# Three chunks of a layer's first MLP product computed by Strassen's scheme with split fp32 operands

## The chip, the core and the metric

The kernel runs on one core of a Trainium2 chip. The metric is the device time of one execution in microseconds (us): the median of the runs shown. TensorE does the matrix products and is fed with weights by a load step of its own (PE and PEld in the profile), VectorE (DVE) and ScalarE (ACT) work element by element, GpSimd (POOL) and SyncE (SP) issue transfers; SP's queue carries nearly all loads of weights.

## The reference

One inference step of a model of two layers. The 640 tokens (512 of a latent grid, 128 of a prompt) have 1024 features. Each layer computes

```python
hn = rmsnorm(x, w0) * (1 + scale1) + shift1
y  = mixer(hn)                       # attention, gated convolution, RG-LRU, pooling; then w_out
x  = x + gate1 * y
hn = rmsnorm(x, w1) * (1 + scale2) + shift2
x  = x + gate2 * (square(relu(hn @ w_mlp1)) @ w_mlp2)
```

with `w_mlp1` of 1024 x 4096 and `w_mlp2` of 4096 x 1024, all in fp32. The modulations (`shift`, `scale`, `gate`) come from products with `w_ada`. The results are the normalized tokens, and the keys, values and states of the prompt.

## The kernel before

Activations lie with features on the 128 partitions and tokens along the row. They are handled in two halves of 320 tokens, A and B (the code's `c`). Products keep fp32 accuracy by splitting each operand x into a rounded part `hi` and the rest `lo = x - hi`, and adding three products: w_hi x_hi + w_lo x_hi + w_hi x_lo. A **group** (line 574) is one output tile of 128 features x 320 tokens: 8 blocks of 128 input features, three matmuls each, 24 in all, in one of two PSUM banks of the pool `gp`. An evacuation (`evac`) follows each group; the next but one group takes the bank.

Weights come as tiles `st` of 512 x 256 (512 KB), loaded by SP into a ring of 3 buffers (`load_next`, line 217). `step` (line 237) turns a tile into a pair: ScalarE casts it to `wh` (line 260), VectorE computes `wl = st - wh` (line 243). Four pairs are held at a time.

The MLP of a layer runs in 4 chunks `q` of 1024 hidden features. Chunk q of the first product, "1" in the names of groups, is 16 groups (4 keys `b` of 256 features, two tiles `mi` each, halves A and B). Its evacuation `evac1` (line 1266) is a relu and a square into `z` (hi) on ScalarE, and a square and a subtraction into `z` (lo) on VectorE (lines 1275 to 1280). Then chunk q of the second product, "2" in the names, is another 16 groups whose evacuation adds to the residual `x` on VectorE (line 1219). So the tensor engine alternates between 1-chunks and 2-chunks.

What engine does what when is settled at build time. Python generators are advanced by `tick` and emit instructions, and a scheduler then sets the order of each engine's instructions by its own estimate, with some raised in priority. At run time each engine works through its list in that order and waits where a semaphore says so; a waiting instruction holds up all that stand behind it on its engine. Names in the rows drop the numbers of buffers.

Of the kernel before, what the change touches and what calls it, by code (L numbers as in the profile page):

```python
# [9 lines left out]
F32 = mybir.dt.float32  # L10
# [29 lines left out]
AP2 = (0, 2, 4, 6, 8)  # L40
AQ = (0, 1, 3, 5)
AP1 = {"xr": (0, 8), "xb": (8, 16)}
RP = 645
XC = 642
UP = 643
# [49 lines left out]
class Slots:  # L95
# [14 lines left out]
    def put(self, *tiles):  # L110
        for t in tiles:
            self.free.append(self.own.pop(id(t))[0])


class Net:
    def __init__(self, tc, es, ins, outs, consts):
        self.tc, self.nc, self.I, self.O = tc, tc.nc, ins, outs
        nc = self.nc
        self.gens = []
        self.c0 = CUT[0]  # L120
        self.const = es.enter_context(tc.tile_pool(name="const", bufs=1))
# [19 lines left out]
        self.stage, self.ready, self.half = {}, {}, None  # L141
        self.ada_acc, self.ada_k = [None, None], 0
        self.setup_consts(consts)

    def setup_consts(self, consts):
        nc, c = self.nc, self.const
        self.cst = c.tile([P, 164], F32, name="cst")
        nc.scalar.dma_start(self.cst, consts[:, 0:164])
        self.ident = self.cst[:, 0:128]
        self.inv = self.cst[:, 128:130]  # L150
        self.edge = self.cst[:, 130:162].rearrange("p (f j) -> p f j", f=2)
        self.consts = consts
        self.sel = c.tile([P, 2], F32, name="sel")
        selv = self.cst[:, 0:128].rearrange("p (j r) -> p r j", j=4)[:, 0:2, :]
# [12 lines left out]
        self.plw = c.tile([P, 2, P], F32, name="plw")  # L167
        self.kcT = c.tile([P, 2, P], F32, name="kcT")
        self.vsb = c.tile([P, 6, 256], F32, name="vsb")
        self.osb = c.tile([P, 2, T], F32, name="osb")  # L170
# [46 lines left out]
    def load_next(self):  # L217
        if self.loaded >= len(self.items):
            return
        kind, src = self.items[self.loaded][:2]  # L220
        nc = self.nc
        t = self.wst.tile([P, 1024], F32, tag="st", name=f"st{self.loaded}")
        if kind == "w":
# [13 lines left out]
    def step(self):  # L237
        nc = self.nc
        if self.half is not None:
            key, st, wh, wl, i = self.half  # L240
            with self.tc.high_priority(offset=self.offw(key)):
                eng = nc.gpsimd if self.booting else nc.vector
                eng.tensor_tensor(wl.rearrange("p k c -> p (k c)"), st,  # L243
                                  wh.bitcast(F32).rearrange("p k c -> p (k c)"), OP.subtract)
            self.ready[key] = (wh, wl)
            self.half = None
            self.load_next()
            return True
        if self.ii >= len(self.items):
            return False  # L250
        it = self.items[self.ii]
        if it[0] == "w":
            if self.live >= 4:
                return False
            self.live += 1
            st = self.stage.pop(self.ii)
            wh = self.whl.tile([P, 4, 256], F32R, tag="wh", name=f"wh{self.ii}")
            wl = self.whl.tile([P, 4, 256], F32R, tag="wl", name=f"wl{self.ii}")
            with self.tc.high_priority(offset=self.offw(it[2])):
                nc.scalar.copy(wh.rearrange("p k c -> p (k c)"), st)  # L260
            self.half = (it[2], st, wh, wl, self.ii)
            self.ii += 1
            return True
        if it[0] == "d":
# [16 lines left out]
        self.load_next()  # L281
        self.load_next()
        if (k, j2) == (KT - 1, 1):
            self.spawn(self.ada_fin(l, s, self.ada_ps), first=True)
        return True

    def ada_dve(self, l, s, g, kp):
        nc = self.nc
# [19 lines left out]
            return True  # L308
        self.stage.pop(self.ii)
        self.ii += 1  # L310
        self.load_next()
        if fin:
            ps = self.psU.get()
            for o in range(2):
# [771 lines left out]
    def layer(self, l, last):  # L1086
# [175 lines left out]
        for q in range(4):  # L1262
# [28 lines left out]
            self.gemm(self.order([(L, "1", q, b) for b in range(4)], lambda i: q == 0 and i == 0), self.mov_h,  # L1291
                      evac1, pre=pre1)
            if q == 0 and not last:
                derive()
            self.tick()
# [241 lines left out]
    def run(self):  # L1537
# [3 lines left out]
        for l in range(DEPTH):  # L1541
# [18 lines left out]
            ni = 0  # L1560
            for q in range(4):
                for b in range(4):
                    it += self.w_items(I["w_mlp1"][l], (L, "1", q, b), 0, 1024 * q + 256 * b)
                    n = 2 if q else AQ[b]
                    it += nxt[ni:ni + n]
                    ni += n
# [43 lines left out]
```

## Time and profile before

| | us |
|---|---|
| median of 3 runs (lowest, highest) | 1478.43 (1477.95, 1479.59) |
| the profiled execution | 1477.53 |
| its span, first to last instruction | 1475.4 |
| VectorE busy in the span | 940.5 (64%) |
| ScalarE busy in the span | 588.2 (40%) |

The profile's page gives for each engine the time in which it was busy and its share of the span. The rows further down come from that page and from questions put to the trace: groups of instructions with their mean time, stretches of time with the busy time of each engine in them, and instructions in order of time with the idle time ahead of each and what ended it.

### The profile page before, as it was taken

How to read it: one execution, taken by the hardware profiler on the slowest of the kernel's cores; microseconds unless marked ns; L12 is line 12 of the kernel's file. 1: busy time of each engine (PE TensorE's matmuls, PEld its weight loads, DVE VectorE, ACT ScalarE, POOL GpSimd, SP SyncE). 2: the span in 40 equal slices, each digit the busy share in tenths (PEclk: the TensorE clock that was granted, in tenths of full speed). 3: DMA queues.
4: the chain of work that ended last, by engine and by line, in shares of the span. 5: the costliest groups of instructions: out<-in, count | busy, mean ns of one | idle time of the engine just before them, and what ended most of it. 6: DMA issues, size and time to landing. Idle time of an engine off the chain costs nothing.

```text
span 1475.4 us, 24595 instructions
## 1 busy us (share of the span) xinstructions
PE 1451.5 (98%) x9991; PEld 1388.8 (94%) x9991; DVE 940.5 (64%) x1846; ACT 588.2 (40%) x1077; POOL 60.9 (4%) x104
## 2 busy tenths in 40 slices
PE   8999999999999999999999999999999999999998
PEld 6877989999999999999999999899999999999997
DVE  5655989898886677766468778848434433433453
ACT  5535784353224123224245578526412312312321
POOL 1221010010000000000002200000000000000000
PEclk9999999999999999999999999999999999999999
DMA  9586112434554444544134411211222122222211
GB/s 332 177 220 185 59 54 88 149 98 157 187 170 130 157 137 137 171 142 129 58 104 123 128 31 57 72 58 58 90 82 86 58 86 75 69 86 64 80 44 72
DMA packets 135960, 164.59 MB, mean 112 GB/s; under 512 B 10212, under 2 KB 111032, under 8 KB 135848
## 3 DMA queue, kind: packets, MB, share of 16 engines
q1 hardware_dynamic: 131256, 156.41, 34.8%
q0 software_dynamic: 4224, 6.45, 1.8%
q8 instruction: 79, 1.29, 0.4%
q14 instruction: 33, 0.27, 0.1%
q10 hardware_dynamic: 368, 0.16, 0.0%
HBM read 150.40 MB, written 3.15 MB: 104 GB/s over the span
## 4 chain that ended last, share of the span: by engine, by line
PE 85%; DVE 6%; issue 4%; DMA 3%; ACT 1%; SPq 0%; DVEq 0%; ACTq 0%; POOLq 0%
PE g_L_1A L583 15%; PE g_L_0A L583 15%; PE g_L_0B L583 14%; PE g_L_1B L583 14%; PE g_L_o_0B L583 1%; PE g_L_o_1B L583 1%; PE g_L_v L1176 1%; PE TB L840 1%; PE U L948 1%; PE S L793 1%; PE g_L_o_0A L583 1%; PE g_L_o_1A L583 1%; PE TA L820 1%; PE U L278 1%; DMA st<-in_w_in 1%
## 5 line engine op out<-in xcount | busy, mean ns | idle before, releaser
L260 ACT CAST wh<-st 128x1024 fp32r<-128x1024 f32 x180 | 188.8, 1049 | 337.4 <-PE g_L_1B L583 275.7
L243 DVE TENSOR_TENSOR wl<-st,wh 128x1024 fp32r<-128x1024 f32 x176 | 215.0, 1222 | 102.8 <-ACT wh L260 102.4
L1279 DVE TENSOR_TENSOR e<-e 128x320 f32<-128x320 f32 x128 | 62.4, 488 | 109.9 <-ACT z L1276 109.5
L583 PE MATMUL g_L_1A<-z,wh 128*128 128x320 f32 (+1 forms) x512 | 121.4, 314 | 0.0
L583 PE MATMUL g_L_0A<-z,wh 128*128 128x320 f32 (+1 forms) x512 | 120.7, 314 | 0.0
L583 PE MATMUL g_L_0B<-z,wh 128*128 128x320 f32 (+1 forms) x512 | 117.2, 309 | 2.3 <-DVE x L1219 2.2
L583 PE MATMUL g_L_1B<-z,wh 128*128 128x320 f32 (+1 forms) x512 | 115.7, 306 | 0.0
L305 DVE SCALAR_TENSOR_TENSOR m<-st,SC,m 128x512 f32<-128x512 f32 x112 | 79.5, 746 | 26.3 <-DMA st<-in_w_ada 26.3
L583 PEld LDWEIGHTS g_L_0B<-z,wh 128*128 128x128 f32 x512 | 87.4, 191 | 2.8 <-DVE x L1219 2.8
L583 PEld LDWEIGHTS g_L_1A<-z,wh 128*128 128x128 f32 x512 | 87.7, 188 | 2.5 <-issue 2.5
L583 PEld LDWEIGHTS g_L_0A<-z,wh 128*128 128x128 f32 x512 | 87.8, 188 | 0.1
L583 PEld LDWEIGHTS g_L_1B<-z,wh 128*128 128x128 f32 x512 | 86.4, 189 | 0.1
L305 DVE SCALAR_TENSOR_TENSOR pt<-st,SC,pt 128x512 f32<-128x512 f32 x112 | 79.9, 745 | 3.4 <-DMA st<-in_w_ada 2.9
L583 PE MATMUL g_L_1A<-hh,wh 128*128 128x320 f32 x256 | 80.0, 313 | 0.0
L583 PE MATMUL g_L_1A<-z,wl 128*128 128x320 f32 (+1 forms) x256 | 79.9, 312 | 0.0
L583 PE MATMUL g_L_0A<-z,wl 128*128 128x320 f32 (+1 forms) x256 | 79.9, 312 | 0.0
L583 PE MATMUL g_L_0A<-hh,wh 128*128 128x320 f32 x256 | 79.5, 311 | 0.2
L583 PE MATMUL g_L_0B<-hl,wh 128*128 128x320 f32 x256 | 79.3, 310 | 0.0
L583 PE MATMUL g_L_1A<-hl,wh 128*128 128x320 f32 x256 | 79.2, 309 | 0.0
L583 PE MATMUL g_L_0A<-hl,wh 128*128 128x320 f32 x256 | 79.1, 309 | 0.0
L583 PE MATMUL g_L_0B<-hh,wh 128*128 128x320 f32 x256 | 79.1, 309 | 0.0
L583 PE MATMUL g_L_1B<-hh,wh 128*128 128x320 f32 x256 | 79.1, 309 | 0.0
(587 smaller groups left out, 3969.9 us busy)
## 6 DMA issues: line engine op xcount, KB each, us to landing
st<-in_w_mlp SPq DMA_DIRECT2D x128, 512.0 KB
st<-in_w_ada SPq DMA_DIRECT2D x80, 512.0 KB
st<-in_w_in SPq DMA_DIRECT2D x36, 512.0 KB
st<-in_w_out SPq DMA_DIRECT2D x16, 512.0 KB
z<-in_w_ada SPq DMA_DIRECT2D x24, 256.0 KB
z<-qk POOLq DMA_DIRECT2D x32, 80.0 KB, 4.4
z<-qk SPq DMA_DIRECT2D x32, 80.0 KB
xt<-in_x_sample SPq DMA_DIRECT2D x4, 512.0 KB
```

What stands on the lines that cost most here:

```text
L243: eng.tensor_tensor(wl.rearrange("p k c -> p (k c)"), st, wh.bitcast(F32).rearrange("p k c -> p (k c)"), OP.subtract)
L260: nc.scalar.copy(wh.rearrange("p k c -> p (k c)"), st)
L278: nc.tensor.matmul(self.ada_ps[32 * g:32 * g + 32, :], self.SC[:, k, :], src[:, (g % 2) * 512:(g % 2 + 1) * 512], start=(k == 0), stop=(k ...
L305: nc.vector.scalar_tensor_tensor(acc[:, 0:512], w, col, acc[:, 0:512], OP.mult, OP.add)
L583: nc.tensor.matmul(pt[:, 0:ncols], w[:, k % 4, sl], r, start=(n == 0), stop=(n == 23))
L793: nc.tensor.matmul(ps[:, o:o + b - a], Q[:, qt * P:(qt + 1) * P], K[:, a:b], start=True, stop=True)
L820: nc.tensor.transpose(ta[:, kt * P:(kt + 1) * P], es[0][:, kt * P:(kt + 1) * P], self.ident)
L840: nc.tensor.matmul(tb[64 * j:64 * j + 64, 0:P], self.vsb[:, kt, (h - 1 + j) * 64:(h + j) * 64], self.pTs[j][:, kt * P:(kt + 1) * P], start ...
L948: nc.tensor.matmul(u[:, 0:321], self.rgw[:, 4 * d + 2 * g + f, :], xc[:, cs], start=True, stop=True)
L1176: nc.tensor.matmul(pt[:, 0:256], a[:, k, ts], b[:, k % 4, :], start=(n == 0), stop=(n == 23))
L1279: nc.vector.tensor_tensor(r[:, 0:n], r[:, 0:n], r[:, 0:n], OP.mult)
```

## The change

In layer 2 the 1-chunks q = 1, 2 and 3 (`FAST`) are computed by Strassen's scheme (Winograd's form). The block of a half chunk, 1024 input features x 512 hidden features x 640 tokens, is cut in two along each dimension. In place of 8 products of half blocks there are 7, numbered `prod`, each of 24 matmuls (2 tiles `mi`, 4 blocks of 128 input features, three matmuls). A half chunk runs them in the order 1, 5, 6, 3, 2, 7, 4.

- **Sums of activations.** While chunk 0 of the second product runs, `sums_gen` makes the four sums and differences of token halves, each split in hi and lo, in buffers that are free at that time: for each of 4 blocks of features 12 instructions on VectorE and 4 on ScalarE.
- **Sums of weights.** Each half chunk loads 7 tiles: A11, A21, A22, A12, B11, B21, B22. Four products take a sum that VectorE adds in place (line 311), and each of the seven operands is split as before (lines 314 and 252).
- **Evacuation.** Products 1, 5 and 6 are copied out of PSUM by ScalarE while their banks go on to accumulate (6 on top of 1; 3 on 5; 7 on 6; 4 on 7); 3, 2 and 7 are added to these copies by VectorE (line 450). The final relu, the two squares and the subtraction follow in `late`. Six banks take part: two of `gp`, the three of the tile `S`, and `TB`.
- **Ring.** Tiles are loaded into 5 buffers. `spent` loads the next tile once the tile five places before it is used up. The scratch memory for transfers that GpSimd issues is set to 8192 bytes per partition.

The core of the diff:

```diff
+WST = 5
+FAST = {(1, 1), (1, 2), (1, 3)}
...
-        self.wst = es.enter_context(tc.tile_pool(name="wst", bufs=3))
+        self.wst = es.enter_context(tc.tile_pool(name="wst", bufs=WST))
...
+    def spent(self, *items):
+        self.gone.update(items)
+        while self.loaded < len(self.items) and (self.loaded < WST or self.loaded - WST in self.gone):
+            self.load_next()
...
+    def sum_and_split(self, it):
...
+        dst, add, prod, done = todo[self.micro]
+        st = self.held[dst][0]
+        if add:
+            nc.vector.tensor_tensor(st, st, self.held[add][0], OP.add)
...
+        nc.scalar.copy(wh.rearrange("p k c -> p (k c)"), st)
+        self.half = ((key + (prod,), 0), st, wh, wl, [self.held.pop(n)[1] for n in done])
...
+    def fast_items(self, w, key, r0, c0):
+        out = []
+        for name, i, j, todo in (("A11", 0, 0, [("A11", None, 1, [])]), ("A21", 1, 0, []),
+                                 ("A22", 1, 1, [("A21", "A22", 5, ["A22"]), ("A11", "A21", 6, ["A21"])]),
+                                 ("A12", 0, 1, [("A11", "A12", 3, ["A11"]), ("A12", None, 2, ["A12"])]),
+                                 ("B11", 0, 0, []), ("B21", 1, 0, [("B11", "B21", 7, ["B11", "B21"])]),
+                                 ("B22", 1, 1, [("B22", None, 4, ["B22"])])):
+            out.append(("x", w[r0 + 512 * j:r0 + 512 * j + 512, c0 + 512 * i:c0 + 512 * i + 256], name, todo, key))
+        return out
...
+    def sums_gen(self):
...
+        for k in range(4):
...
+            full(b12, k, B)
+            full(w, k, A)
+            tt(t1, w, b12, OP.subtract)
+            yield
+            split(T1[k], t1)
+            full(b22, k + 4, B)
+            yield
+            tt(w, b22, b12, OP.subtract)
+            split(T3[k], w)
...
+    def fast_mlp1(self, l, q, put):
...
+        pairs = [(g[0], g[1]), (S[:, 0:512], S[:, 512:1024]), (S[:, 1024:1536], tb)]
...
+            def late():
+                if sign:
+                    nc.scalar.activation(v, v, AF.Relu, scale=sign)
+                nc.scalar.activation(hi, v, AF.Square)
+                nc.scalar.activation(v, v, AF.Square)
+                yield
+                nc.vector.tensor_tensor(lo, v, hi.bitcast(F32), OP.subtract)
...
+        for b in range(2):
+            Y, Z, X = pairs[b % 3], pairs[(b + 1) % 3], pairs[(b + 2) % 3]
+            r = u2 = None
+            for prod, bank in ((1, Y), (5, Z), (6, Y), (3, Z), (2, X), (7, Y), (4, Y)):
...
+                fresh = prod in (1, 5, 2)
+                for mi in range(2):
...
+                    for k in range(4):
+                        hi, lo = self.Tsum[prod][k]
+                        for w, x in ((wh, hi), (wl, hi), (wh, lo)):
+                            nc.tensor.matmul(bank[mi][:, 0:HC], w[:, k, sl], x, start=(fresh and n == 0), stop=(n == 11),
+                                             skip_group_check=not fresh)
+                            n += 1
...
+                        if prod in (1, 5, 6):
+                            nc.scalar.copy(half({1: t1, 5: t5, 6: u2}[prod], mi), p)
+                        elif prod == 4:
+                            nc.scalar.activation(half(r, mi), p, AF.Relu, scale=-1.0)
+                        else:
+                            nc.vector.tensor_tensor(half(r, mi), p, half({3: u2, 2: t1, 7: t5}[prod], mi), OP.add)
...
-    nc = bacc.Bacc("TRN2", target_bir_lowering=False, num_devices=1)
+    nc = bacc.Bacc("TRN2", target_bir_lowering=False, num_devices=1, dynamic_dma_scratch_size=8192)
```

The places in the order of instructions of which the prediction speaks are three. On VectorE, from the end of chunk 0 of the second product into chunk 1 of the first, before the change:

```order
L1219 SCALAR_TENSOR_TENSOR x_76<-g_L1_2_3_0_1B_11711,mod1_92,x_76 128x128
L243 TENSOR_TENSOR wl215_11775<-st215_11519,wh215_11774 128x1024 [waits DMAHW5_49,Activation_49]
L1279 TENSOR_TENSOR e1_226_11771<-e1_226_11771 128x320 [waits Activation_49]
L1280 TENSOR_TENSOR z11_206_11770<-e1_226_11771,z13_205_11769 128x320 [waits DVE_49]
L1279 TENSOR_TENSOR e0_227_11809<-e0_227_11809 128x320 [waits Activation_49]
L1280 TENSOR_TENSOR z6_208_11808<-e0_227_11809,z2_207_11807 128x320 [waits DVE_49]
L1279 TENSOR_TENSOR e2_228_11839<-e2_228_11839 128x320 [waits Activation_49]
L1280 TENSOR_TENSOR z11_206_11770<-e2_228_11839,z13_205_11769 128x320 [waits DVE_49]
```

and with the change from the second weight tile that is split in the fast chunk on; the names end in the product, `wl215_2` is the `wl` of product 2, `st220` and `st221` are A21 and A22 of the second half chunk, `st223` and `st224` its B11 and B21, and `e1_235` takes product 3:

```order
L252 TENSOR_TENSOR wl215_2_11890<-st215_11589,wh215_2_11889 128x1024 [waits PE_49,Activation_49]
L252 TENSOR_TENSOR wl217_7_11924<-st216_11628,wh217_7_11923 128x1024 [waits PE_49,Activation_49]
L311 TENSOR_TENSOR st220_11907<-st220_11907,st221_11943 128x1024 [waits DMAHW3_49,DMAHW2_49,DVE_49]
L252 TENSOR_TENSOR wl218_4_11966<-st218_11872,wh218_4_11965 128x1024 [waits DMAHW0_49,PE_49,Activation_49]
L450 TENSOR_TENSOR e1_235_11938<-S_36_11819,e2_234_11904 128x320 [waits PE_49]
L411 TENSOR_TENSOR z11_206_11941<-e1_235_11938,z13_205_11940 128x320 [waits Activation_49]
L450 TENSOR_TENSOR e1_235_11938<-S_36_11819,e2_234_11904 128x320 [waits PE_49]
L450 TENSOR_TENSOR e0_236_11984<-TB_72_11820,pt1_65_11823 128x320 [waits PE_49]
L252 TENSOR_TENSOR wl219_1_12007<-st219_11874,wh219_1_12006 128x1024 [waits DMAHW1_49,Activation_49]
L311 TENSOR_TENSOR st223_11987<-st223_11987,st224_12141 128x1024 [waits DMAHW6_49,DMAHW5_49,DVE_49]
```

Where evacuation arithmetic and two subtractions for weights stood, there now stand two additions that wait for transfers (DMAHW) ahead of the sums that empty PSUM.

On TensorE in the same half chunk, with the change. The tile `S` holds three banks; the first rows are the end of product 5's first tile (bank 0 of `S`), then come four matmuls of product 6 (two of them in one row), then product 5's second tile (bank 1 of `S`):

```order
L432 MATMUL S_36_11819<-osb_2_11272,wl214_5_11732 128x320
L432 MATMUL S_36_11819<-vsb_2_11273,wh214_5_11731 128x320
L432 MATMUL f1_0_11821<-qk_6_11274,wh214_6_11816 128x320 [waits Activation_49]
L432 MATMUL f1_0_11821<-qk_6_11274,wl214_6_11817 128x320
L432 MATMUL f1_0_11821<-qk_6_11274,wh214_6_11816 128x320 x2
L432 MATMUL S_36_11819<-osb_2_11272,wh214_5_11731 128x320 [waits Activation_49]
L432 MATMUL S_36_11819<-osb_2_11272,wl214_5_11732 128x320
```

Twelve matmuls of one output tile no longer stand in one piece: the second tile of product 5 waits for ScalarE's copy of the first, which lies in another bank of the same `S`, and four matmuls of product 6 have been put ahead of it.

On VectorE in chunk 0 of the second product, where before only evacuations (line 1219, now 1404) and subtractions for weights stood, with the change the sums of activations and of weights (`st213`, `st214` are A21 and A22) stand between evacuations:

```order
L381 TENSOR_TENSOR e2_231_11464<-e2_231_11464 128x320 [waits DVE_49]
L354 TENSOR_TENSOR e0_230_11463<-hh_77,hl_78 128x320 [waits DVE_49]
L363 TENSOR_TENSOR hl_78<-e0_230_11463,hh_77 128x320 [waits Activation_49]
L360 SCALAR_TENSOR_TENSOR qk_6_11274<-e2_231_11464,qk_6_11274 128x320 [waits Activation_49]
L385 TENSOR_TENSOR e0_230_11463<-e2_231_11464,e0_230_11463 128x320 [waits DVE_49]
L311 TENSOR_TENSOR st213_11442<-st213_11442,st214_11482 128x1024 [waits DMAHW4_49,DMAHW3_49]
L1404 SCALAR_TENSOR_TENSOR x_76<-g_L1_2_1_0_1A_11468,mod1_92,x_76 128x320 [waits PE_49]
L363 TENSOR_TENSOR m5_123_11278<-e0_230_11463,m3_121_11276 128x320 [waits Activation_49]
```

Between the evacuations of two groups there are now some seven to nine instructions.

## Rows read from the trace of the kernel before

**Rows 1.** the page: TensorE's busy time, and the chain that ended last.
```profile
PE 1451.5 (98%) x9991; PEld 1388.8 (94%) x9991; DVE 940.5 (64%) x1846; ACT 588.2 (40%) x1077; POOL 60.9 (4%) x104
PE 85%; DVE 6%; issue 4%; DMA 3%; ACT 1%; SPq 0%; DVEq 0%; ACTq 0%; POOLq 0%
```

**Rows 2.** the chain in time: start us, us, engine, tile, line, matmuls.
```profile
1123.22 3.51 PE g_L_0A L583 x24
...
1176.02 3.52 PE g_L_1B L583 x24
...
1404.19 4.20 PE g_L_0A L583 x24
```

**Rows 3.** stages: us, busy us (instructions) per engine, clock, DMA share, GB/s.
```profile
1067.00:1123.00 56.00, 56.00 (x386) 56.00 (x385) 19.32 (x33) 9.09 (x10) 0.00 (x0) 1.00 0.24 76
1123.00:1179.50 56.50, 56.50 (x387) 56.50 (x386) 25.02 (x41) 21.38 (x38) 0.00 (x0) 1.00 0.24 75
```

**Rows 4.** ScalarE groups, 1123 to 1404 us: busy us, mean ns, idle.
```profile
L260 ACT CAST wh<-st 128x1024 fp32r<-128x1024 f32 x40 | 41.9, 1047 | 104.4 <-PE g_L_1B L583 104.4
L1276 ACT ACTIVATE z<-e 128x320 fp32r<-128x320 f32 x47 | 22.2, 472 | 1.1
L1275 ACT ACTIVATE e<-g_L_0A 128x320 f32<-128x320 f32 x12 | 5.2, 437 | 23.4 <-PE g_L_0A L583 23.4
```

**Rows 5.** VectorE groups, 1123 to 1404 us, the same columns.
```profile
L243 DVE TENSOR_TENSOR wl<-st,wh 128x1024 fp32r<-128x1024 f32 x41 | 50.2, 1225 | 39.1 <-ACT wh L260 39.1
L1280 DVE TENSOR_TENSOR z<-e,z 128x320 fp32r<-128x320 f32 x47 | 23.1, 492 | 1.6
L1219 DVE SCALAR_TENSOR_TENSOR x<-g_L_0A,mod,x 128x320 f32<-128x320 f32 x8 | 4.4, 550 | 7.1 <-PE g_L_0A L583 7.1
```

**Rows 6.** ScalarE in order of time: start us, us, instruction, idle before.
```profile
1016.81 0.44 ACT L1275 ACTIVATE e<-g_L_0A 128x320 f32<-128x320 f32 x1 [1.44 <-PE g_L_0A L583]
1017.14 0.43 ACT L1275 ACTIVATE e<-g_L_1A 128x320 f32<-128x320 f32 x1
...
1137.67 1.04 ACT L260 CAST wh<-st 128x1024 fp32r<-128x1024 f32 x1
1138.60 0.47 ACT L1276 ACTIVATE z<-e 128x320 fp32r<-128x320 f32 x1
```

**Rows 7.** SP's queue in order of time, two loads of 512 KB.
```profile
1123.85 0.37 SPq L224 DMA_DIRECT2D st<-in_w_mlp  x1
1125.60 0.37 SPq L224 DMA_DIRECT2D st<-in_w_mlp  x1
```

**Rows 8.** short stretches around these loads, columns as in Rows 3.
```profile
1124.50:1127.00 2.50, 2.50 (x19) 2.50 (x18) 1.07 (x1) 0.23 (x1) 0.00 (x0) 1.00 0.71 219
1127.00:1130.50 3.50, 3.50 (x26) 3.50 (x25) 0.98 (x2) 0.89 (x3) 0.00 (x0) 1.00 0.49 150
1130.50:1132.00 1.50, 1.50 (x12) 1.50 (x11) 0.70 (x2) 0.70 (x2) 0.00 (x0) 1.00 0.00 0
```

**Rows 9.** TensorE's waits, 60 to 485 us: total us, times, longest.
```profile
PE g_L_0B L583 <- DVE x L1219: 2.2, 1, 2.2
PE S L793 <- DMA z<-qk: 1.0, 1, 1.0
PE g_L_xr_0A L583 <- DVE wl L243: 0.8, 1, 0.8
```

**Rows 10.** the wait of VectorE ahead of the longest of these.
```profile
DVE e L438 <- DMA e<-in_diff_lambda: 4.1, 1, 4.1
```

**Rows 11.** stretches around these waits, columns as in Rows 3.
```profile
60.00:200.00 140.00, 137.14 (x925) 111.52 (x923) 100.62 (x210) 82.39 (x174) 20.87 (x40) 1.00 0.54 149
364.00:367.00 3.00, 0.75 (x4) 0.60 (x4) 3.00 (x11) 0.00 (x0) 0.00 (x0) 0.97 0.20 65
367.00:371.00 4.00, 4.00 (x19) 4.00 (x19) 4.00 (x13) 1.04 (x1) 0.00 (x0) 0.59 0.56 171
```

More of the change, by code (lines that the diff above doesn't have):

```diff
@@ L141, in __init__ @@
         self.stage, self.ready, self.half = {}, {}, None
+        self.held, self.micro, self.gone = {}, 0, set()
         self.ada_acc, self.ada_k = [None, None], 0
@@ L168, in setup_consts @@
         self.kcT = c.tile([P, 2, P], F32, name="kcT")
-        self.vsb = c.tile([P, 6, 256], F32, name="vsb")
-        self.osb = c.tile([P, 2, T], F32, name="osb")
+        self.vsbS = Slots(c, ["vsb"], [P, 6, 256])
+        self.osbS = Slots(c, ["osb"], [P, 2, T])
+        self.vsb, self.osb = self.vsbS.get(), self.osbS.get()
         self.hsel = c.tile([P, 2], F32, name="hsel")
@@ L246, in step @@
             self.half = None
-            self.load_next()
+            self.spent(*i)
             return True
@@ L260, in step @@
                 nc.scalar.copy(wh.rearrange("p k c -> p (k c)"), st)
-            self.half = (it[2], st, wh, wl, self.ii)
+            self.half = (it[2], st, wh, wl, [self.ii])
             self.ii += 1
             return True
+        if it[0] == "x":
+            return self.sum_and_split(it)
         if it[0] == "d":
@@ L285, in step @@
         return True
+    def sum_and_split(self, it):
+        nc = self.nc
+        _, _, name, todo, key = it
+        if self.micro == 0 and name not in self.held:
+            self.held[name] = (self.stage.pop(self.ii), self.ii)
+        if not todo:
+            self.ii += 1
+            return self.step()
+        if self.live >= 4:
+            return False
+        self.live += 1
+        dst, add, prod, done = todo[self.micro]
+        st = self.held[dst][0]
+        if add:
+            nc.vector.tensor_tensor(st, st, self.held[add][0], OP.add)
+        wh = self.whl.tile([P, 4, 256], F32R, tag="wh", name=f"wh{self.ii}_{prod}")
+        wl = self.whl.tile([P, 4, 256], F32R, tag="wl", name=f"wl{self.ii}_{prod}")
+        nc.scalar.copy(wh.rearrange("p k c -> p (k c)"), st)
+        self.half = ((key + (prod,), 0), st, wh, wl, [self.held.pop(n)[1] for n in done])
+        self.micro += 1
+        if self.micro == len(todo):
+            self.micro = 0
+            self.ii += 1
+        return True
@@ new lines, in fast_mlp1, with finish @@
+    def fast_mlp1(self, l, q, put):
+        nc = self.nc
+        self.until(lambda: self.summed and self.psS.ok() and self.psB.ok() and self.pt.ok(2), "sums")
+        S, tb = self.psS.get(), self.psB.get()
+        g = [self.gp.tile([P, 512], F32, tag="g", name=f"f{q}_{i}") for i in range(2)]
+        pairs = [(g[0], g[1]), (S[:, 0:512], S[:, 512:1024]), (S[:, 1024:1536], tb)]
+        t1, t5 = self.pt.get(), self.pt.get()
+        half = lambda t, mi: t[:, HC * mi:HC * mi + HC]
+        left = {}
+        def finish(m, c, r, mi, sign):
+            hi, lo = put(m, c)
+            v = half(r, mi)
+            def late():
[3 more added lines that the diff above has]
+                nc.scalar.activation(v, v, AF.Square)
+                yield
+                nc.vector.tensor_tensor(lo, v, hi.bitcast(F32), OP.subtract)
+                left[id(r)] -= 1
+                if not left[id(r)]:
+                    self.e.put(r)
+            self.spawn(late(), first=True)
+        for b in range(2):
+            Y, Z, X = pairs[b % 3], pairs[(b + 1) % 3], pairs[(b + 2) % 3]
+            r = u2 = None
+            for prod, bank in ((1, Y), (5, Z), (6, Y), (3, Z), (2, X), (7, Y), (4, Y)):
+                key = ((f"L{l}", "1s", q, b, prod), 0)
+                self.until(lambda: key in self.ready, "fast weights")
+                wh, wl = self.ready[key]
+                fresh = prod in (1, 5, 2)
+                for mi in range(2):
+                    sl = slice(mi * P, mi * P + P)
+                    n = 0
+                    for k in range(4):
[4 more added lines that the diff above has]
+                            n += 1
+                    p = bank[mi][:, 0:HC]
+                    lowm, highm = 2 * b + mi, 4 + 2 * b + mi
+                    if mi == 0 and prod in (6, 3, 2, 7, 4):
+                        self.until(lambda: self.e.ok(), "fast e")
+                        if prod == 6:
+                            u2 = self.e.get()
+                        else:
+                            r = self.e.get()
+                            left[id(r)] = 2
+                    with self.tc.high_priority(offset=OFF):
+                        if prod in (1, 5, 6):
+                            nc.scalar.copy(half({1: t1, 5: t5, 6: u2}[prod], mi), p)
+                        elif prod == 4:
+                            nc.scalar.activation(half(r, mi), p, AF.Relu, scale=-1.0)
+                        else:
+                            nc.vector.tensor_tensor(half(r, mi), p, half({3: u2, 2: t1, 7: t5}[prod], mi), OP.add)
+                    if prod in (3, 2, 7, 4):
+                        m, c = {3: (lowm, 1), 2: (lowm, 0), 7: (highm, 1), 4: (highm, 0)}[prod]
+                        finish(m, c, r, mi, {7: -1.0, 4: None}.get(prod, 1.0))
+                    if prod == 3 and mi == 1:
+                        self.e.put(u2)
+                    if mi == 1:
+                        self.ready.pop(key)
+                        self.live -= 1
+                    self.tick()
+        self.pt.put(t1, t5)
+        self.psS.put(S)
+        self.psB.put(tb)
@@ L287, in ada_dve, with sums_done @@
+    def sums_done(self):
+        o, v, qk, ms = self.sum_own
+        self.osbS.put(o)
+        self.vsbS.put(v)
+        self.qk.put(qk)
+        self.m.put(*ms)
+        self.vsb, self.osb = self.vsbS.get(), self.osbS.get()
     def ada_dve(self, l, s, g, kp):
@@ L310, in ada_dve @@
         self.ii += 1
-        self.load_next()
+        self.spent(self.ii - 1)
         if fin:
@@ L1289, in pre1, with put @@
                     self.until(lambda: (l, 1, 1) in self.norm_done, "norm2B")
-            self.gemm(self.order([(L, "1", q, b) for b in range(4)], lambda i: q == 0 and i == 0), self.mov_h,
-                      evac1, pre=pre1)
+            def put(m, c, q=q):
+                if (m, 0) not in h or h[m, 0][2] != q:
+                    h[m, 0] = (self.z.get(F32R), self.z.get(F32R), q)
+                return h[m, 0][0][:, self.cs(c)], h[m, 0][1][:, self.cs(c)]
+            if (l, q) in FAST:
+                self.fast_mlp1(l, q, put)
+            else:
+                self.gemm(self.order([(L, "1", q, b) for b in range(4)], lambda i: q == 0 and i == 0), self.mov_h,
+                          evac1, pre=pre1)
+            if q == 0 and (l, 1) in FAST:
+                self.summed = False
+                self.spawn(self.sums_gen())
+            if q == 3 and (l, 3) in FAST:
+                self.until(lambda: not self.gens, "last sums")
+                self.sums_done()
             if q == 0 and not last:
```

52 lines of the change are left out of this document (48 added, 4 removed).

## The prediction

> **What bounds the kernel now.** I read the page first. TensorE is busy for 1451.5 of 1475.4 us, and 85% of the chain that ended last is its own [rows 1]; the other engines have room. So time is gained by issuing fewer matmuls, as long as nothing makes TensorE wait. The chain in order of time shows how they run in layer 2: groups of 24 in 3.51 to 3.52 us, one upon the other, so 3.52 / 24 = 0.1467 us a matmul; chunk 1 of the first product goes from 1123.22 to 1179.54, and the last chunk ends at 1404.19 [rows 2]. The table by stage (busy columns: PE, PEld, DVE, ACT, POOL) has TensorE without a gap at clock 1.00, with VectorE busy 25.0 us and ScalarE 21.4 in such a chunk, and 19.3 and 9.1 in a chunk of the second product [rows 3]. Here weights, evacuations and loads are all hidden.
>
> I make the sum against the profiled execution, 1477.53 us, of which 2.1 lie outside the span. The median is 0.9 above it.
>
> **Removed.** Three chunks of 16 groups have 3 x 384 = 1152 matmuls. Strassen takes 3 x 2 x 7 products of 24, or 1008. So 144 go, at 0.1467 us: -21.1 us. Columns, operand type and loads per matmul stay, so I take the same price for the rest. A fast chunk needs 49.3 us where it needed 56.3.
>
> **Added beside TensorE.** In a fast chunk VectorE has 14 subtractions for weights and 8 additions, 22 x 1.225; 12 evacuations with an addition, priced as the nearest reading of PSUM, 0.55; and 16 subtractions of 0.49 [rows 5]. That is 27.0 + 6.6 + 7.9 = 41.5 us. ScalarE has 14 casts of 1.05, 16 readings of PSUM at 0.44, and 44 relus and squares at 0.47 [rows 4]: 14.7 + 7.0 + 20.8 = 42.5 us. Instructions that don't depend on each other start a little closer than they last (0.33 apart for 0.44, 0.93 for 1.04) [rows 6], so both engines are some 80 to 85% full in 49.3 us. They keep up on the average, but little is free, and order decides. Loads double: 14 tiles of 512 KB in 49.3 us are 149 GB/s where 75 was; from 60 to 200 us the kernel moves 149 GB/s at a DMA share of 0.54 [rows 11], so the engines for it are there.
>
> **Where TensorE will wait in a fast chunk.** I follow the order of the first half chunk from its first matmul, with half a product at 12 x 0.1467 = 1.76 us and 0.2 us from the last matmul to the next engine.
>
> The three banks of `S` are one tile, and the order shows that a matmul into one bank waits for the copy out of the one before. For product 5's second tile that costs 0.1 us: four matmuls of product 6 (0.59) cover a copy that takes 0.2 + 0.44.
>
> For product 3's second tile it is longer. VectorE must first have emptied product 3's first tile, and ahead of that evacuation stands the addition of `st220` and `st221`. The buffer of `st221` comes free when `wl215_2` is made. ScalarE copies product 1's two tiles with a cast between them (2.0 to 4.1) and casts product 2's weight (to 5.1); VectorE subtracts (to 6.35); only now SP issues the load. In the trace two loads go out at 1123.85 and 1125.60 [rows 7], and the transfer engines are idle again after 1130.5 [rows 8], so the second takes up to 4.9 us. It lands at 11.25; the addition ends at 12.5, the next subtraction at 13.7, the evacuation at 14.2. TensorE arrives there after 94 matmuls and the first wait, at 13.9: 0.3 us. The next such place, product 2's second tile, comes out at 0.1, and the evacuations of product 7, which product 4 needs, at 0 to 0.1, behind an addition for `st223` and `st224` that ends at 19.5.
>
> In the second half chunk ScalarE is late. It has twelve instructions for products 2, 7 and 4 and the cast for product 6 ahead of its copy of product 1's first tile, which begins near 28.0 with TensorE waiting from 27.65: 0.65 us. Five later places cost 0.05 to 0.2 each, and the passage into the second product 0.2 to 0.3, since matmuls of its first group are put between those of products 7 and 4. Together 0.1 + 0.3 + 0.1 + 0.1 + 0.65 + 0.45 = 1.7 us a chunk, three times: +5.1.
>
> Bounds: 0 if the matmuls put in between cover it all. Above, the nearest case is the one at 364 us: VectorE held 4.1 us by a transfer [rows 10], an evacuation late behind it, TensorE 2.25 us idle [rows 9], and then four us at a mean clock of 0.59 [rows 11]; 4 x (1 - 0.59) is another 1.6. So up to 3.9 for one; one a chunk makes 11.7. I take 5.1, nearer to zero, since the loads have a measured duration.
>
> **The chunk of the second product with the sums.** 48 small instructions at 0.49 and three additions of weights add 27 us to VectorE's 19.3 in 56. From its start to the evacuation of the ninth group VectorE has about 42 small instructions, 4 subtractions and an addition of 1.2, and 8 evacuations at 0.55 to 0.68: 19 + 5 + 1.2 + 5 = 30 us in the 32 us that TensorE needs. An evacuation may be 3.5 us late before a bank is missed. By the order, the eighth and the tenth are late by 0.3 to 0.6. I take +1.0, with 0 and 3 as ends.
>
> **The ring.** Five buffers concern all loads, and the scheduler has put the first attention stage in another order. There TensorE's waits for weights and transfers are 0.8 and 1.0 [rows 9], so at most some 2 us can go, and a changed order can cost as much. The idle 2.25 us at 364 stay: VectorE still stands behind the same small transfer. I take 0, from -1.5 to +1.5.
>
> **The sum.** 1477.5 - 21.1 + 5.1 + 1.0 = 1462.5 us.
>
> [...] The trace has single waits only, and none under 1 us that moved the clock; a run of them it does not show.
>
> **Rivals.**
> - *The fill covers everything.* For it: the scheduler has put other matmuls into each of these waits. Against it: the half chunks leave ScalarE and VectorE about 4 us of slack, and two loads can only start when a subtraction is over. 1477.5 - 21.1 = 1456.4, with -1 of the ring 1455. Chance 0.2.
> - *The additions wait longer for their loads.* With a third load in flight each landing is 1 to 2 us later, and both places in the half chunk slip by as much, as there is no slack behind the first: 2.5 to 3.5 us more a chunk, so 1470 to 1473. For it: loads double, and no row shows three of them at once. Against it: 149 GB/s at a share of 0.54. Chance 0.2.
> - *Slower: the clock falls in each half chunk.* One place, the addition that waits for `st221` (in the second half chunk ScalarE's backlog ahead of the copy). If TensorE idles as long as at 364, each half chunk pays 3.9 us; six are 23.4 and 1477.5 - 21.1 + 23.4 + 1.0 = 1480.8. It decides from 3.4 us a half chunk on. [...] For it: the same chain of transfer, VectorE, evacuation did it once. Against it: there VectorE was held for 4.1 us, and here, by the steps above, for about 1. Chance 0.05.
> - *The change doesn't do what it says* (the fast products cost more per matmul, or the waits eat just the gain): 1475 to 1480, chance 0.03.
>
> **Numbers.** The forecast, 1458 to 1468, has the remaining 0.52. The range that leaves out 2 in 10 goes from 1456 to 1471. A measurement tells 0.2%, 3 us, from no change. The first three cases are all faster by more: 0.92. Of the rest 0.03 is the same and 0.05 slower.
>
> **What will show it.** 9991 - 144 = 9847 matmuls; the three 1-chunks 51 us each instead of 56.3, at clock 1.00; VectorE 940 + 70 = about 1010 us busy (18 subtractions, 24 additions, 48 sums, 36 evacuations more, 48 squares less); in the fast chunks waits of TensorE under 0.7 us, the longest for ScalarE's copy of product 1 and for VectorE's evacuation of product 3; VectorE idle for about 1 us ahead of line 311, for a load, in each first half chunk. It is wrong if TensorE's waits in a fast chunk pass 4 us, if the clock falls there, or if the time before 1000 us moves by more than 2.

## The result, and the profile after

The changed kernel takes 1459.65 us in the median (four executions, 1458.18 to 1461.10) against 1479.01 us before (four executions here; the three shown ahead of the prediction had 1478.43); the ratio is 0.9875 (95% interval 0.9862 to 0.9887). The forecast was 1462.5, with a range of 1458 to 1468. The profiled execution took 1458.18 us with a span of 1456.4. First the page, its lines on busy time and on the chain that ended last, which answer to [rows 1]:

```profile
PE 1434.4 (98%) x9847; PEld 1367.7 (94%) x9847; DVE 998.6 (69%) x1924; ACT 643.7 (44%) x1195; POOL 60.9 (4%) x104
PE 88%; DVE 5%; DMA 3%; ACT 2%; issue 1%; SPq 0%; DVEq 0%; ACTq 0%
```

The 144 matmuls are gone (9847 where there were 9991). Next the chain in order of time (start us, us, engine, tile, line, matmuls). In the changed kernel the three fast chunks begin at the rows with `f`:

```profile
1060.46 3.51 PE g_L_0A L768 x24
...
1116.47 3.53 PE f L432 x24
...
1225.47 3.52 PE f L432 x24
...
1333.14 3.53 PE f L432 x24
```

and the chunks that correspond to the second and the third in the kernel before, with 1123.22 for the first [rows 2]:

```profile
1235.55 3.51 PE g_L_0A L583 x24
...
1347.88 3.51 PE g_L_0A L583 x24
```

From such starts, and the two spans for the end, the whole difference can be laid out by stage:

| stage | before, us | after, us | difference | forecast |
|---|---|---|---|---|
| up to the first fast chunk | 1123.22 | 1116.47 | -6.75 | 0 (ring), +1.0 (sums) |
| chunk 1, and the 2-chunk behind it | 112.33 | 109.00 | -3.33 | -7.04 + 1.7 |
| chunk 2, and the 2-chunk behind it | 112.33 | 107.67 | -4.66 | -7.04 + 1.7 |
| chunk 3, to the end | 127.5 | 123.3 | -4.3 | -7.04 + 1.7 |
| sum | 1475.4 | 1456.4 | -19.0 | -15.0 |

So a third of the gain lies ahead of the fast chunks, and those give 12.3 of the 21.1 us that their missing matmuls are worth: 8.8 are lost in them, 3.7, 2.4 and 2.8. The stretches of the changed kernel (us, busy us and instructions of PE, PEld, DVE, ACT, POOL, then clock, DMA share, GB/s) answer to [rows 3]: the 2-chunk with the sums, the first fast chunk with what follows it up to an even group boundary, the rest of that 2-chunk, the second fast chunk.

```profile
1060.50:1116.50 56.00, 56.00 (x386) 56.00 (x385) 40.15 (x79) 15.41 (x25) 0.00 (x0) 1.00 0.27 85
1116.50:1176.00 59.50, 58.76 (x385) 56.33 (x384) 37.79 (x52) 39.50 (x75) 0.00 (x0) 1.00 0.41 127
1176.00:1225.50 49.50, 49.50 (x338) 49.26 (x338) 19.58 (x31) 7.35 (x7) 0.00 (x0) 1.00 0.27 83
1225.50:1284.00 58.50, 58.28 (x385) 56.19 (x384) 37.82 (x52) 39.51 (x75) 0.00 (x0) 1.00 0.42 129
```

In the first line TensorE has no gap although VectorE does twice the work, and it runs 386 matmuls in 56.00 us as it did before [rows 3]: the sums cost nothing. In the second, 385 matmuls at 0.1467 would be 56.5 us and take 59.5, with the clock at 1.00. Yet the list of TensorE's waits from 1050 us to the end (us in total, times, longest) has no more than this for all three fast chunks:

```profile
PE S L432 <- ACT pt L446: 0.7, 3, 0.2
PE f L432 <- DVE e L450: 0.4, 1, 0.4
```

The rest has to be read from the starts. TensorE in order of time (start us, us, instruction) at a place that the list does not have:

```profile
1150.33 0.31 PE L432 MATMUL TB<-hl,wh 128*128 128x320 f32 x1
1150.48 0.31 PE L432 MATMUL TB<-hh,wh 128*128 128x320 f32 x1
1150.72 0.41 PE L432 MATMUL S<-qk,wh 128*128 128x320 f32 x1
1150.97 0.30 PE L432 MATMUL S<-qk,wl 128*128 128x320 f32 x1
1151.11 0.46 PE L432 MATMUL S<-qk,wh 128*128 128x320 f32 x2
```

Starts are 0.15 us apart, then 0.24, 0.25, and 0.14 again: this matmul and the one behind it come 0.1 us late each. A row lasts 0.31 us, twice the pitch, so a start that is late by less than 0.16 us leaves no gap in the list. What it waited for is on ScalarE (the same columns, with the idle time ahead), a copy of another bank of `S` that ended at 1150.67:

```profile
1150.24 0.43 ACT L446 COPY pt<-S 128x320 f32<-128x320 f32 x1 [0.85 <-PE S L432]
```

I added up what the intervals have above 0.147 us at every such place. The first fast chunk has 14 places of any size with 3.2 us together; eleven of them, with 2.3, stand where the matmuls go on to `S`, and wait for the reading of a bank of this tile, nearly always another bank than their own. In the second and third chunk such places take 2.0 and 2.1 us.

### The profile page after: what moved, and what is told of

Same layout as the page of the kernel before. It is cut to its first block, busy times and chain, and to the rows that moved or that the text cites. A ratio compares the mean times of both kernels' runs of the same rounds, so it can differ in the third digit from the quotient of the medians.

```text
span 1456.4 us, 24564 instructions
## 1 busy us (share of the span) xinstructions
PE 1434.4 (98%) x9847; PEld 1367.7 (94%) x9847; DVE 998.6 (69%) x1924; ACT 643.7 (44%) x1195; POOL 60.9 (4%) x104
## 4 chain that ended last, share of the span: by engine, by line
PE 88%; DVE 5%; DMA 3%; ACT 2%; issue 1%; SPq 0%; DVEq 0%; ACTq 0%
PE g_L_0A L768 13%; PE g_L_1A L768 13%; PE g_L_0B L768 12%; PE g_L_1B L768 12%; PE S L432 4%; PE g_L_o_0B L768 2%; PE g_L_o_1B L768 2%; PE g_L_v L1361 2%; PE g_L_o_0A L768 2%; DMA st<-in_w_mlp 2%; PE g_L_o_1A L768 2%; PE f L432 2%; PE TB L1025 1%; PE S L978 1%; PE U L1133 1%; PE U L289 1%
## 5 line engine op out<-in xcount | busy, mean ns | idle before, releaser
L252 DVE TENSOR_TENSOR wl<-st,wh 128x1024 fp32r<-128x1024 f32 x194 | 236.8, 1222 | 107.8 <-ACT wh L269 69.8
L269 ACT CAST wh<-st 128x1024 fp32r<-128x1024 f32 x156 | 163.6, 1049 | 225.8 <-PE g_L_1B L768 195.1
L768 PE MATMUL g_L_1A<-z,wh 128*128 128x320 f32 (+1 forms) x512 | 122.1, 315 | 0.0
L768 PE MATMUL g_L_1B<-z,wl 128*128 128x320 f32 (+1 forms) x256 | 78.7, 307 | 0.0
L768 PE MATMUL g_L_0B<-z,wl 128*128 128x320 f32 (+1 forms) x256 | 78.5, 307 | 0.0
L684 ACT ACTIVATE e<-x 128x320 f32<-128x320 f32 (+2 forms) x56 | 26.4, 471 | 117.1 <-DVE x L1404 116.7
L314 ACT CAST wh<-st 128x1024 fp32r<-128x1024 f32 x42 | 44.1, 1050 | 76.4 <-PE g_L_1B L768 69.8
L1464 DVE TENSOR_TENSOR e<-e 128x320 f32<-128x320 f32 x80 | 39.0, 488 | 48.1 <-ACT z L1461 47.9
L987 DVE TENSOR_REDUCE mx<-S 128x2 f32<-128x1280 f32 x32 | 47.6, 1487 | 19.7 <-PE S L978 19.6
L991 ACT ACTIVATE e<-S,mx 128x640 f32<-128x640 f32 x64 | 50.9, 801 | 6.5 <-DVE mx L988 5.8
L1404 DVE SCALAR_TENSOR_TENSOR x<-g_L_0B,mod,x 128x192 f32<-128x192 f32 (+1 forms) x64 | 21.3, 375 | 45.2 <-PE g_L_0B L768 44.8
```

What stands on the lines that cost most here:

```text
L252: eng.tensor_tensor(wl.rearrange("p k c -> p (k c)"), st, wh.bitcast(F32).rearrange("p k c -> p (k c)"), OP.subtract)
L684: nc.scalar.activation(s[:, 0:n], self.x[:, k, cs], AF.Square)
L768: nc.tensor.matmul(pt[:, 0:ncols], w[:, k % 4, sl], r, start=(n == 0), stop=(n == 23))
L987: nc.vector.tensor_reduce(mx[:, 0:2], ps[:, 128:1408].rearrange("p (s k) -> p s k", s=2), AX.X, OP.max)
L991: nc.scalar.activation(es[s], ps[:, 128 + 640 * s:768 + 640 * s], AF.Exp, bias=mx[:, 2 + s:3 + s], scale=sc, accum_out=self.sm[:, i, s:s + 1])
L1404: nc.vector.scalar_tensor_tensor(self.x[:, m, a:b], pt[:, a - a0:b - a0], self.mod[l][:, gate + m, st:st + 1], self.x[:, m, a:b], OP.mult, ...
```

## Experiments

Each kernel was timed beside the kernel before on the same chip, whose median there was 1478.18 us (experiments 1, 4 and 5, and three tiles in 2) or 1478.37 (3, 6 and 7, and four tiles). The changed kernel was not timed again there, so it is best compared with these runs by the ratios; its own is 0.9875 (0.9862 to 0.9887).

**1. The ring alone.** All of the change but the fast chunks:

```diff
-FAST = {(1, 1), (1, 2), (1, 3)}
+FAST = set()
```

> Ring of five tiles and the smaller scratch as in the changed kernel, no chunk by Strassen's scheme. Theory A: the 6.75 us that the changed kernel is ahead of the one before when the first fast chunk begins come from the order that goes with the ring; then 1479.0 - 6.75 = 1472.3 us (1471 to 1474), VectorE's wait of 4.1 us for in_diff_lambda is near 1.3, and chunk 1 of layer 2's first product starts at 1116.5. Rival B: the stretches at half clock (at 367 and 954 us before, at 94 after) come and go from one execution to the next; then only the wait of 2.2 us is gone for good, and the median is 1476 to 1478. Rival C: the ring does nothing and the median is 1479.

Measured: 1472.61 us, ratio 0.9952 (0.9937 to 0.9967), so 4.9 to 9.3 us less than before. Theory A's number for the time holds, but not its start of chunk 1: in the profiled execution that is at 1119.56, 3.7 us earlier than before and not 6.7. Rival C falls. Rival B is half true, and the trace shows how. VectorE's wait for in_diff_lambda is down to 1.7 us, and of the two stretches at clock 0.50 in the kernel before (366.9 to 370.2 us and 954.0 to 957.3) the first is gone, but others are there. Three stretches of this run, in columns as above:

```profile
219.80:223.20 3.40, 3.40 (x15) 3.40 (x14) 2.58 (x5) 1.14 (x2) 0.76 (x1) 0.50 0.14 30
362.00:366.00 4.00, 4.00 (x29) 4.00 (x29) 4.00 (x13) 0.00 (x0) 0.00 (x0) 1.00 0.44 131
950.30:953.60 3.30, 3.30 (x14) 3.30 (x14) 1.24 (x3) 0.53 (x1) 0.00 (x0) 0.50 0.24 85
```

of the kernel before:

```profile
954.00:957.30 3.30, 3.30 (x14) 3.30 (x14) 1.25 (x3) 0.53 (x1) 0.00 (x0) 0.50 0.16 55
```

and of the changed kernel, behind the same place of the program:

```profile
949.00:952.40 3.40, 3.40 (x26) 3.38 (x25) 1.68 (x4) 1.10 (x3) 0.00 (x0) 1.00 0.17 58
```

In all three kernels TensorE idles 2.2 us just before, for the same wait; twice the clock then falls to 0.50, and once it stays at 1.00. At 0.50, 14 matmuls run in 3.3 us where the changed kernel runs 26 in 3.4, so a fall costs some 1.5 us. As much of the 6.75 us between the two profiled executions arises at this place and is of this kind, and the ring's own part is better taken from the medians, 5.6. Most of what the profiled execution with five tiles is ahead arises at the other place: the hundred matmuls around 364 us take 14.6 us in it and 18.6 in the kernel before.

**2. Three and four tiles, without fast chunks.** `WST = 3` and `WST = 4` in the kernel of experiment 1.

> As the run with five tiles and no fast chunk, but with three tiles: what is left of the change is its bookkeeping, which loads the next tile when the tile three places before it is used up. Theory A (the number of buffers counts): as before, 1478 to 1480 us, with VectorE's wait of 4 us for in_diff_lambda and TensorE's of 2.2 us behind it. Rival (any other order of emission does it, whatever the ring): 1472 to 1475.

> As the runs with rings of three (1478.8 us) and five (1472.6) without fast chunks, with four tiles. Theory A: a further buffer lets loads start earlier, so four lies between: 1474 to 1477. Rival B: it is the order that the scheduler happens to find that counts, and four is outside: below 1472 or above 1479.

Measured: three tiles 1478.76 us, ratio 1.0003 (0.9993 to 1.0012); four 1474.66, ratio 0.9977 (0.9965 to 0.9990). The bookkeeping and the smaller scratch memory, which all these runs have, do nothing for the time, and by the medians each further buffer gives 2 to 4 us. That does not clear the order as a cause, since it changes with each size. And A's detail for three tiles was wrong: the profiled execution does not have the stall near 364 either, but comes to this place 4 us later. VectorE's wait there (us in total, times, longest):

```profile
DVE e L623 <- DMA e<-in_diff_lambda: 1.6, 1, 1.6
```

So this execution is without the stall, and by its median the run is no faster: the stall alone does not account for the 5.6 us of five tiles.

**3. The load of in_diff_lambda.** In the kernel before, GpSimd issues it once a transpose has read the tile that it goes to. It is moved to the other parameters of layer 2 (the main lines):

```diff
+        if l == 1:
...
+            q.dma_start(rows[:, P:2 * P], dl.to_broadcast([P, P]))
         return lambda: self.derive_params(l, rows, q)
...
```

> The kernel before, with one load moved: GpSimd loads layer 2's in_diff_lambda along with the other parameters near 300 us, into unused columns of their tile, and not at 356.7 after a transpose of that tile. Theory A: VectorE's wait of 4.1 us for this load, TensorE's of 2.2 us behind it and the half clock after it go, which is 3.9 of the 5.6 us that the ring of five gained alone: 1478.2 - 3.9 = 1474.3 us (1473 to 1476). Rival B: another late instruction takes its place there, or the place was worth nothing over many executions: 1477 to 1479.

The place itself does what A says. TensorE in the stretches of [rows 11] is now without a gap, at clock 1.00, and the hundred matmuls around 364 us take 15.0 us for 18.6:

```profile
364.00:367.00 3.00, 3.00 (x23) 3.00 (x22) 3.00 (x10) 0.00 (x0) 0.00 (x0) 1.00 0.54 172
367.00:371.00 4.00, 4.00 (x29) 4.00 (x29) 4.00 (x13) 1.08 (x2) 0.00 (x0) 1.00 0.46 137
```

The median is 1475.48 us (twelve executions), but the ratio, 0.9987 (0.9972 to 1.0001), holds both no gain and the 3.9 us. By its time this run decides nothing, so what the stall is worth over many executions stays open. In the changed kernel the same load is issued at 353.10 where before it was at 356.66; TensorE's 2.2 us of [rows 9] are gone from its list of waits. Here are GpSimd's issue there, and VectorE's wait, which was 4.1 [rows 10]:

```profile
353.10 0.58 POOL L620 DMA_DIRECT2D e<-in_diff_lambda  x1 [49.27 <-PE g_L_1B L768]
...
356.54 0.23 DVE L623 TENSOR_TENSOR e<-e 128x64 f32<-128x64 f32 x1 [1.33 <-DMA e<-in_diff_lambda]
```

**4. A tile for each bank.** In place of two banks of `S` the fast chunks take `U` and `TA`, which are free at that time:

```diff
-        pairs = [(g[0], g[1]), (S[:, 0:512], S[:, 512:1024]), (S[:, 1024:1536], tb)]
+        pairs = [(g[0], g[1]), (S[:, 0:512], u), (ta, tb)]
...
```

> The changed kernel with each of the six PSUM banks of a fast chunk in a tile of its own (TA and U in place of two banks of S). Theory A: a matmul into one bank of S waits for the copy out of another, and each such wait costs 0.1 to 0.5 us although the list of waits shows hardly any; by the intervals between matmuls these places take 2.3, 2.0 and 2.0 us in the three fast chunks, so 1459.6 - 6 = 1453.5 us (1452 to 1455). Rival B: ScalarE and VectorE are late with these copies anyway, and the wait only moves to the next use of the same bank: 1458 to 1460.

Measured: 1452.90 us, ratio 0.9822 (0.9808 to 0.9836). Theory A holds within a microsecond; B falls. The late starts at `S` and the banks in its place, eleven in the first chunk of the changed kernel, are gone. (Without these waits the scheduler also leaves the matmuls of a half product in one piece, so order and waits changed together.) The chain shows the half products following each other without a gap (12 x 0.1467 = 1.76), and the starts of the three fast chunks:

```profile
1114.80 3.52 PE f L433 x24
1118.32 1.77 PE S L433 x12
1120.09 1.76 PE U L433 x12
1121.85 3.53 PE f L433 x24
...
1220.91 3.53 PE f L433 x24
...
1326.92 3.53 PE f L433 x24
```

106.1 and 106.0 us from one to the next, where 105.3 is what the removed matmuls allow, and 121.3 to the end of the span: 2.3 us are lost in all, not 8.8. What is left is 0.3 to 0.4 us in each chunk where product 4 waits for VectorE's evacuation of product 7, and 0.3 at the first group of the second product. This version beats both kernels.

**5. Without the sums of weights.** The first line of the edit, with two of the four sums; the other two go in the same way:

```diff
-                                 ("A22", 1, 1, [("A21", "A22", 5, ["A22"]), ("A11", "A21", 6, ["A21"])]),
+                                 ("A22", 1, 1, [("A21", None, 5, ["A22"]), ("A11", None, 6, ["A21"])]),
...
```

> The changed kernel without the four additions of weight tiles in each half chunk (the products take unsummed tiles; loads, casts and subtractions stay). Theory A: an addition that waits for its load, and stands ahead of an evacuation on VectorE, costs TensorE 0.2 us at product 3 and 0.5 us at product 4 in the first fast chunk and 0.1 in the third, and nothing elsewhere: 1458.6 us (1457.5 to 1459.5). Rival B: the additions and their loads are behind most of the 2.3 to 3.1 us that a fast chunk loses: 1453 to 1455.

Measured: 1457.53 us, ratio 0.9857 (0.9844 to 0.9870), 2 to 3 us less than the changed kernel: twice what A says, and short of B. The intervals of the two ratios overlap, so the places in the trace must carry this: the late starts of the first fast chunk add up to 1.9 us for 3.2, of the second to 1.9 for 2.4. A had left out one place. In all three chunks the 0.5 us for ScalarE's copy of product 1 in the second half chunk go too, because VectorE and with it the casts run earlier: the copy begins 26.9 us behind the chunk's first matmul in place of 28.5. The 0.2 us at each other bank of `S` stay, as A has it.

**6. Four tiles, with fast chunks** (`WST = 4` in the kernel of experiment 4).

> own_banks with a ring of four tiles instead of five. Theory A: the additions can wait some 2 us longer for their loads before TensorE notices, so the fast chunks stay within 2 us of own_banks (324.8 us from their start to the end), and only the time before them changes with the order. Rival B: VectorE already waits up to 4.7 us for loads there, one buffer less delays each by another 2 to 4 us, and each of six half chunks loses as much: 12 us or more.

Measured: 1456.09 us, ratio 0.9864 (0.9841 to 0.9886). The starts of its fast chunks:

```profile
1118.29 3.51 PE f L433 x24
...
1224.12 3.51 PE f L433 x24
...
1329.76 3.51 PE f L433 x24
```

105.8 and 105.6 us apart, and 122.1 to the end of the span of 1451.9. That is 333.6 us from their start to the end, against 333.4 in experiment 4 (the 324.8 of the expectation is an error): theory A. For the fast chunks four buffers are as good as five; what five gain, 3.2 us by the medians, they gain before them.

**7. The sums of weights on GpSimd**, with a tile for each bank:

```diff
-            nc.vector.tensor_tensor(st, st, self.held[add][0], OP.add)
+            nc.gpsimd.tensor_tensor(st, st, self.held[add][0], OP.add)
...
```

> A tile of its own for each bank, as in own_banks, and the additions of weights on GpSimd. Theory A: what own_banks still loses in a fast chunk, 0.3 to 0.4 us where product 4 waits for VectorE's evacuation of product 7 and 0.3 at the first group of the second product, stands behind additions on VectorE that wait for loads; off VectorE they cost nothing, 24 x 2.4 us are hidden on GpSimd: 1452.9 - 1.5 = 1451.4 us (1450.5 to 1452.5). Rival B: an addition takes GpSimd 2.4 us where VectorE took 1.2, the sums come late or VectorE runs slower beside it, and TensorE waits for weights: 1454 to 1460.

Measured: 1464.20 us, ratio 0.9909 (0.9887 to 0.9932), 11 us more than with the sums on VectorE: rival B, beyond its range, but TensorE waits for evacuations by VectorE and not for weights. In the profiled executions the first fast chunk begins 3.4 us later than in experiment 4, and the three chunks cost 2.0, 1.9 and 6.7 us more. In groups (instructions, busy us, mean ns, idle), VectorE's subtractions of weights and of squares and its additions out of PSUM, from 1110 to 1400 us with the sums on GpSimd:

```profile
L252 DVE TENSOR_TENSOR wl<-st,wh 128x1024 fp32r<-128x1024 f32 x60 | 79.5, 1325 | 71.0 <-ACT wh L314 53.5 <-ACT wh L269 17.5
L412 DVE TENSOR_TENSOR z<-e,z 128x320 fp32r<-128x320 f32 x48 | 37.8, 816 | 4.0 <-ACT e L410 4.0
L451 DVE TENSOR_TENSOR e<-f,pt 128x320 f32<-128x320 f32 x12 | 5.8, 483 | 0.0
```

and of experiment 4:

```profile
L412 DVE TENSOR_TENSOR z<-e,z 128x320 fp32r<-128x320 f32 x48 | 21.9, 484 | 1.5 <-ACT e L410 1.5
L451 DVE TENSOR_TENSOR e<-f,pt 128x320 f32<-128x320 f32 x12 | 5.8, 485 | 0.0
```

A subtraction of two SBUF operands takes 816 ns on the mean where it took 484; an addition with one operand in PSUM takes 483 and 485. In order of time one sees the longest of them, two subtractions of VectorE from 1352.95 beside two additions of GpSimd from 1352.76, and behind them the evacuation out of `f` that TensorE needs:

```profile
1352.95 5.12 DVE L412 TENSOR_TENSOR z<-e,z 128x320 fp32r<-128x320 f32 x2
1358.00 0.48 DVE L451 TENSOR_TENSOR e<-TB,pt 128x320 f32<-128x320 f32 x1
1358.40 1.21 DVE L252 TENSOR_TENSOR wl<-st,wh 128x1024 fp32r<-128x1024 f32 x1
1359.53 0.48 DVE L451 TENSOR_TENSOR e<-f,pt 128x320 f32<-128x320 f32 x1
```

```profile
1352.76 4.96 POOL L311 TENSOR_TENSOR st<-st,st 128x1024 f32<-128x1024 f32 x2 [4.32 <-issue]
```

```profile
1360.16 0.61 PE L433 MATMUL f<-m,wh 128*128 128x320 f32 x1 [4.94 <-DVE e L451]
```

TensorE waits 4.9 us for VectorE there, and from 1357.9 to 1364.6 the granted clock is 0.50, where from 1353.0 to 1357.8 it was 1.00. VectorE's two subtractions last to 1358.07, GpSimd's two additions to 1357.72. Two additions of VectorE out of PSUM were no slower beside GpSimd: at 1131.33 and 1132.29, during GpSimd's addition from 1130.28 to 1133.68, they took 0.48 and 0.49 us. Why the one kind of VectorE's instructions is held up there and the other is not, no run shows.

## Why the prediction was right, and where not

- **Removed, -21.1.** Right. 9847 matmuls, groups of 24 in 3.52 us, and in experiment 4 the fast chunks give 18.8 of the 21.1 us.
- **The first half chunk, followed by hand.** Right almost to the instruction. VectorE idles 0.82 us ahead of the first addition (about 1 was said), for a load that goes out at 1122.68, 6.2 us behind the first matmul (6.35). The addition ends at 1129.02, which is 12.55 us behind the first matmul (12.5), and the evacuation of product 3 at 1130.55, 14.1 behind it (14.2). The rows of VectorE:

```profile
1127.79 1.23 DVE L311 TENSOR_TENSOR st<-st,st 128x1024 f32<-128x1024 f32 x1 [0.82 <-DMA st<-in_w_mlp]
1128.93 1.22 DVE L252 TENSOR_TENSOR wl<-st,wh 128x1024 fp32r<-128x1024 f32 x1
1130.07 0.48 DVE L450 TENSOR_TENSOR e<-S,e 128x320 f32<-128x320 f32 x1
```

  The place cost 0.4 us in the first chunk, 0.2 and 0.3 in the others (0.3 was said); ScalarE's late copy of product 1 in the second half chunk begins 28.5 us behind the first matmul (28.0) and cost 0.5 (0.65).
- **"1.7 us a chunk".** The mechanism was right, the term too small: 3.7, 2.4 and 2.8 us were lost. The working itself gives more than it took: five places of 0.05 to 0.2 and a passage of 0.2 to 0.3 are 0.45 to 1.3, and the sum has the lower end. Places that were costed at 0, 0.05 or 0.1, because hardly anything was late there, cost 0.1 to 0.2, since the next matmul comes 0.1 late as well; the second half chunk has six of them. And product 4, which waits for product 7's evacuation, cost 0.6 in the first chunk where 0 to 0.1 was said. That evacuation stood behind an addition that waited 1.14 us for its load and ended 20.9 us behind the first matmul, not 19.5:

```profile
1136.12 1.23 DVE L311 TENSOR_TENSOR st<-st,st 128x1024 f32<-128x1024 f32 x1 [1.14 <-DMA st<-in_w_mlp]
1138.06 0.48 DVE L450 TENSOR_TENSOR e<-f,pt 128x320 f32<-128x320 f32 x1
```

```profile
1138.69 0.38 PE L432 MATMUL f<-m,wh 128*128 128x320 f32 x1 [0.36 <-DVE e L450]
```

  "TensorE's waits pass 4 us in a fast chunk" did not come true.
- **The sums, +1.0.** The value was 0, its lower end.
- **The ring, 0 from -1.5 to +1.5.** This step failed. "The idle 2.25 us at 364 stay" was argued from VectorE's order, where the waiting instruction had not moved; in the changed kernel GpSimd issues the load 3.6 us sooner, VectorE's wait is 1.3 us and not 4.1, and the stall is gone. Alone the ring gives 5.6 us by the medians. The profiled executions put most of it at this stall; but with three tiles the stall is gone too and nothing is gained, and experiment 3 decides nothing, so the cause of the 5.6 us stays open. The forecast's own sign of error, more than 2 us before 1000, came true.
- **The sum** came out near, 1462.5 for 1459.65, because the time ahead of the fast chunks (-6.75 in the profiled execution, where +1.0 was said for the sums and 0 for the ring) outweighed what the chunks lost beyond the forecast (+3.7). That two errors of opposite sign cancel is luck. With the ring at 0 as forecast, and all else as measured, the time would be near 1465, still within the range.
- **Rivals.** The time alone, 1459.65, lies about as near to the rival "the fill covers everything" (1455 to 1456.4) as to the forecast; the table by stage decides, with 8.8 us lost in the fast chunks, of which experiment 4 takes back all but 2.3. The additions' waits for loads cost clearly more than the forecast at one place, ahead of product 4 in the first chunk: 0.5 us, where the rival has 2.5 to 3.5 in every chunk. One buffer less costs the fast chunks nothing (experiment 6). The slower case did not occur, but experiment 7 shows its chain at one place, with GpSimd in place of a transfer at its head: VectorE held for 5 us, an evacuation late, TensorE idle for 4.9, the clock behind it at 0.50 for 1.00.
- **VectorE's busy time.** It has 78 instructions more, as counted in the forecast, but 998.6 us where about 1010 was said: an evacuation with an addition takes 0.48 us and not 0.55, and instructions that follow each other overlap (1128.93 + 1.22 is past 1130.07 in the rows above).
- **Many short waits.** The changed kernel has the run of short waits that the trace of before lacked, 11 to 14 a chunk, and its clock stays at 1.00 in all three chunks.

## What to carry to other kernels

Where several PSUM banks lie in one tile, the first matmul of a run into one bank waited here for the readers of the others; give each bank that is emptied on its own a tile of its own (here 6.7 us by the medians, 6.5 in the fast chunks of the profiled executions). Read short waits from the starts of matmuls, not from the list of waits. When a change alters an order or a ring for the whole program, cost that apart, on all queues, and measure it alone: here it was a third of the gain, and why is not fully known.

## What the runs showed of the hardware

- A matmul held for a moment costs more than the moment: at 1150.72 in the changed kernel its start and the next are 0.24 and 0.25 us after the one before, for 0.147, so 0.2 us are lost for a hold of 0.1.
- TensorE idle for the same 2.2 us lowered its clock in some executions and not in others: to 0.50 in the kernel before (954.0 to 957.3 us) and in experiment 1 (950.3 to 953.6), while it stayed at 1.00 in the changed kernel (949.0 to 952.4). Seventeen executions of the kernel before ran from 1475.65 to 1481.72 us, and 23 on another chip from 1472.50 to 1480.88; single profiles of such kernels should not be compared to better than some 4 us.
- GpSimd's addition of 128x1024 takes 2.56 us on the mean (VectorE's 1.22) and holds up VectorE's subtractions of two SBUF operands beside it: two of them, 0.48 us each alone, took 5.12. VectorE's additions out of PSUM were not held up (483 ns on the mean, 485 in experiment 4; 0.48 and 0.49 us for the two at 1131.33 and 1132.29, during an addition of GpSimd).
